# Attention in a two-layer hybrid block: scores by alternating PE row tiles, values stationary with a channel-major output, softmax divided before its transposes

## The chip, the cores and the metric

The program runs on one core of a Trainium2 chip. The metric is the device time of one execution in microseconds, the median of several runs. The engines that matter here are TensorE (PE: matmuls and transposes; PEld: its weight loads), VectorE (DVE), ScalarE (ACT) and GpSimd (POOL). Each engine works through its own list of instructions in a fixed order and waits on semaphores for the others. Matmul results go to PSUM, in banks of 512 fp32 values for each of 128 partitions.

## The reference, cut to what matters

Two layers, each a feed-forward block, a mixer with four branches, and a second feed-forward block, for 256 tokens (two blocks of 128). Two of the four branches are attention with 8 heads of 64 value channels: `mla` (96 channels in q and k, causal) and `dsa` (64 channels, one k and v shared by all heads, keys picked by an indexer). All data are fp32.

```python
def causal_dense_attention(q, k, v, scale):
    def block(args):
        s = jnp.einsum('bqhd,bshd->bhqs', qb, k).astype(jnp.float32) * scale
        s = jnp.where(kpos[None, :] <= qpos[:, None], s, -jnp.inf)
        p = jax.nn.softmax(s, axis=-1).astype(v.dtype)
        return jnp.einsum('bhqs,bshd->bqhd', p, v)
...
def dsa_branch(q, k, v, q_idx, k_idx, w_idx, cs_main, cs_idx, qk_gain):
        rel = jax.nn.relu(jnp.einsum('bqhd,bsd->bqhs', qib, k_idx).astype(jnp.float32))
        score = jnp.einsum('bqh,bqhs->bqs', wib.astype(jnp.float32), rel)
        _, sel = lax.top_k(score, topk)
        s = jnp.einsum('bqhd,bqkd->bhqk', qb, k_sel).astype(jnp.float32) * DSA_HEAD_DIM ** -0.5
        p = jax.nn.softmax(s, axis=-1).astype(v.dtype)
        return jnp.einsum('bhqk,bqkd->bqhd', p, v_sel)
...
        ys = [y_a, y_b, y_c, y_d]
        merged = gates[:, :, 0] * (y_a @ w_branch[l, 0])
        for n in range(1, N_BRANCH):
            merged = merged + gates[:, :, n] * (ys[n] @ w_branch[l, n])
```

## The kernel before, in words

Weights come from HBM in pieces of up to 512 KB (class `W`: tile `raw`, one DMA on SP's queue). ACT rounds a piece to fp32r (`hi_genexpr`, L232), DVE forms the rest (`lo_genexpr`, L103, 128x1024 elements), and every large product is three fp32r matmuls hi*hi, lo*hi, hi*lo (L244 to L246 for 256 columns, L239 to L241 for the token-major ones). Attention itself is plain fp32: one such matmul is carried out by PE in two passes, and each pass is one record in the trace.

A tile scheduler with priorities, and a table of stages, decide the order on each engine. The gate products (`ps_up_gate`) and the products with `w_branch` (`ps_up_merge`) are large matmuls that need no attention result of the moment, and they are laid between the steps of attention as filler; only the merges of `yT_dsa` and `yT_mla` wait for attention.

In each layer `attend` is called six times: for `mla` with four heads at a time (hh 0 and 1) and for `dsa` with eight heads, each for the two token blocks (tb 0 sees 128 keys, tb 1 sees 256). It works in sets of one PSUM bank, 512 score columns: four heads of 128 keys or two heads of 256. There are 12 sets in a layer. A set is:

- mask and scores on PE into a bank of `acc` (L1105, L1107; `dsa` uses 64-row tiles of the array, even heads the upper, odd heads the lower one),
- the row maximum on DVE (L1109, `mmx` or `dmx`), the exponential on ACT with its row sum (L112, `p_attend`),
- four transposes on PE (L1118, `ps_tp_attend`), copied to SBUF by ACT (L116),
- the product with the values (L1121, `ps_ms_attend`): the transposed probabilities are loaded as weights, the 64 value columns move.

After its sets, `attend` takes reciprocals of the sums and scales the token-major output (L1123 and a DVE multiply, `p_attend<-ps_ms_attend`), `y_trans` transposes it (L1133, `ps_tp_y_trans`), and it is split into hi and lo parts (`yT_mla`, `yT_dsa`). `dsa_index` forms the indexer's scores with four 32-row tiles (L1190), ACT takes relu, DVE adds the heads up.

Before the scores, k of `mla` is normalised: its sum of squares (`mkss`), a power on POOL (L321, `mkr`), two small multiplies and one of 128x512 on DVE (`s5p_mla<-...mkr_mla`), then transposes on PE (L1346). `dsc_dsa` is a similar scale for `dsa`, with a POOL step (L321) between two DVE instructions (L109, L1231).

## Time and profile before

| | before |
|---|---|
| median of 3 runs (range) | 1520.54 us (1517.99 to 1522.41) |
| profiled execution | 1519.11 us |
| its span, first to last instruction | 1517.3 us |
| granted clock of TensorE, mean | 0.982 |
| PE busy | 1439.0 us, 95% |
| DVE busy | 1167.0 us, 77% |
| ACT busy | 771.3 us, 51% |

The profiled execution is 1.8 us longer than its span and 1.4 us below the median. Attention of the first layer lies between about 433 and 529 us of the span, that of the second between about 1170 and 1266 us; both have the same structure. A timeline row gives the start, the time from the first to the last record of a run of like instructions, and in brackets the idle time of the engine ahead of it with what ended it; the step from one row's start to the next one's is what the work took.

### The profile page before, as it was taken

How to read it: one execution, taken by the hardware profiler on the slowest of the kernel's cores; microseconds unless marked ns; L12 is line 12 of the kernel's file. 1: busy time of each engine (PE TensorE's matmuls, PEld its weight loads, DVE VectorE, ACT ScalarE, POOL GpSimd, SP SyncE). 2: the span in 40 equal slices, each digit the busy share in tenths (PEclk: the TensorE clock that was granted, in tenths of full speed). 3: DMA queues.
4: the chain of work that ended last, by engine and by line, in shares of the span. 5: the costliest groups of instructions: out<-in, count | busy, mean ns of one | idle time of the engine just before them, and what ended most of it. 6: DMA issues, size and time to landing. Idle time of an engine off the chain costs nothing.

```text
span 1517.3 us, 26622 instructions
## 1 busy us (share of the span) xinstructions
PE 1439.0 (95%) x10342; PEld 1288.4 (85%) x10342; DVE 1167.0 (77%) x2003; ACT 771.3 (51%) x1223; POOL 63.6 (4%) x75
## 2 busy tenths in 40 slices
PE   8899998899989999999989998999999999999998
PEld 4588887799878897999979897889988889789997
DVE  3699978789787477988787887678987845866655
ACT  4444446644465545444454445467455655544442
POOL 0000000001010000000010000000200100000000
PEclk9999999999999999999999999999999999999999
DMA  9788888786335265899978878754642425567762
GB/s 288 232 294 285 291 258 259 203 232 172 96 102 140 70 206 175 289 320 323 321 250 257 277 244 273 229 135 135 178 132 90 124 83 158 162 212 225 235 207 98
DMA packets 241703, 313.24 MB, mean 206 GB/s; under 512 B 27704, under 2 KB 168872, under 8 KB 241576
## 3 DMA queue, kind: packets, MB, share of 16 engines
q1 hardware_dynamic: 241576, 311.53, 66.0%
q8 instruction: 81, 1.33, 0.4%
q14 instruction: 46, 0.38, 0.1%
HBM read 310.41 MB, written 1.07 MB: 205 GB/s over the span
## 4 chain that ended last, share of the span: by engine, by line
PE 62%; DVE 19%; DMA 7%; issue 5%; ACT 5%; POOL 2%; SPq 0%; POOLq 0%; DVEq 0%; ACTq 0%
DVE lo_genexpr L103 7%; PE ps_up_up_half L244 6%; PE ps_up_up_half L245 6%; PE ps_up_up_half L246 6%; PE ps_acc_down_proj L241 3%; PE ps_acc_down_proj L240 3%; PE ps_acc_down_proj L239 3%; DMA raw_init<-in_ffn_w_dram 3%; DMA raw_ada<-in_ada_w_dram 3%; PE ps_up_gate L244 3%; PE ps_up_gate L246 3%; PE ps_up_gate L245 2%; ACT hi_genexpr L232 2%; PE ps_up_merge L245 2%; PE ps_up_merge L244 2%
## 5 line engine op out<-in xcount | busy, mean ns | idle before, releaser
L232 ACT CAST hi_genexpr<-raw_init 128x1024 fp32r<-128x1024 f32 (+2 forms) x430 | 441.1, 1028 | 504.6 <-DMA raw_init<-in_ffn_w_dram 120.5
L103 DVE TENSOR_TENSOR lo_genexpr<-raw_init,hi_genexpr 128x1024 fp32r<-128x1024 f32 (+2 forms) x430 | 511.5, 1192 | 162.9 <-ACT hi_genexpr L232 155.4
L244 PE MATMUL ps_up_up_half<-uh_new_u,hi_genexpr 128*128 128x256 f32 x1216 | 339.0, 279 | 3.3 <-DVE p_silu_cols L106 2.6
L246 PE MATMUL ps_up_up_half<-uh_new_u,lo_genexpr 128*128 128x256 f32 x1216 | 337.0, 278 | 0.2 <-DVE lo_genexpr L103 0.2
L245 PE MATMUL ps_up_up_half<-ul_new_u,hi_genexpr 128*128 128x256 f32 x1216 | 337.1, 277 | 0.0
L244 PEld LDWEIGHTS ps_up_up_half<-uh_new_u,hi_genexpr 128*128 128x128 f32 x1216 | 228.5, 188 | 9.3 <-issue 7.0
L245 PEld LDWEIGHTS ps_up_up_half<-ul_new_u,hi_genexpr 128*128 128x128 f32 x1216 | 228.5, 188 | 1.4
L246 PEld LDWEIGHTS ps_up_up_half<-uh_new_u,lo_genexpr 128*128 128x128 f32 x1216 | 228.5, 188 | 0.8 <-DVE lo_genexpr L103 0.8
L106 DVE SCALAR_TENSOR_TENSOR acc_ada<-raw_ada,c_col_tile_trunk,acc_ada 128x1024 f32<-128x1024 f32 x105 | 134.4, 1280 | 28.7 <-DMA raw_ada<-in_ada_w_dram 28.3
L244 PE MATMUL ps_up_gate<-uh_new_u,hi_genexpr 128*128 128x256 f32 x512 | 145.3, 284 | 0.0
L245 PE MATMUL ps_up_gate<-ul_new_u,hi_genexpr 128*128 128x256 f32 x512 | 144.1, 281 | 0.0
L246 PE MATMUL ps_up_gate<-uh_new_u,lo_genexpr 128*128 128x256 f32 x512 | 143.6, 281 | 0.0
L239 PE MATMUL ps_acc_down_proj<-hi_genexpr,yT_mul_cols 128*128 128x512 f32 x288 | 115.7, 402 | 0.0
L241 PE MATMUL ps_acc_down_proj<-hi_genexpr,yT_mul_cols 128*128 128x512 f32 x288 | 115.6, 402 | 0.0
L240 PE MATMUL ps_acc_down_proj<-lo_genexpr,yT_mul_cols 128*128 128x512 f32 x288 | 115.3, 401 | 0.1
L244 PEld LDWEIGHTS ps_up_gate<-uh_new_u,hi_genexpr 128*128 128x128 f32 x512 | 96.5, 188 | 2.2 <-issue 1.5
L246 PEld LDWEIGHTS ps_up_gate<-uh_new_u,lo_genexpr 128*128 128x128 f32 x512 | 96.6, 189 | 0.5 <-issue 0.4
L245 PEld LDWEIGHTS ps_up_gate<-ul_new_u,hi_genexpr 128*128 128x128 f32 x512 | 96.5, 188 | 0.1
L239 PEld LDWEIGHTS ps_acc_down_proj<-hi_genexpr,yT_mul_cols 128*128 128x128 f32 x288 | 54.8, 190 | 13.3 <-issue 1.6
L240 PEld LDWEIGHTS ps_acc_down_proj<-lo_genexpr,yT_mul_cols 128*128 128x128 f32 x288 | 54.8, 190 | 12.8 <-DVE lo_genexpr L103 0.6
L241 PEld LDWEIGHTS ps_acc_down_proj<-hi_genexpr,yT_mul_cols 128*128 128x128 f32 x288 | 54.8, 190 | 12.6
L239 PE MATMUL ps_up_tok_gemm<-hi_genexpr,uh_new_u 128*128 128x424 f32 (+2 forms) x88 | 34.0, 386 | 2.2 <-ACT gt_gate L112 2.2
(476 smaller groups left out, 2750.7 us busy)
## 6 DMA issues: line engine op xcount, KB each, us to landing
raw_init<-in_ffn_w_dram SPq DMA_DIRECT2D x240, 512.0 KB
raw_ada<-in_ada_w_dram SPq DMA_DIRECT2D x128, 512.0 KB
raw_init<-in_w_in_dram SPq DMA_DIRECT2D x96, 512.0 KB
raw_init<-in_w_branch_dram SPq DMA_DIRECT2D x32, 512.0 KB
raw_init<-in_ffn_w_dram SPq DMA_DIRECT2D x36, 256.0 KB
raw_init<-in_w_out_dram SPq DMA_DIRECT2D x16, 512.0 KB
s5p_load<-in_ada_w_dram SPq DMA_DIRECT2D x16, 256.0 KB
s5p_load<-in_ada_w_dram SPq DMA_DIRECT2D x8, 512.0 KB
```

What stands on the lines that cost most here:

```text
L103: eng.tensor_tensor(o, x, y, op)
L106: V.scalar_tensor_tensor(o, x, s, y, op0, op1)
L232: S.copy(self.hi, self.raw)
L239: T.matmul(o, xh, wh, start=first, stop=False)
L240: T.matmul(o, xh, wl, start=False, stop=False)
L241: T.matmul(o, xl, wh, start=False, stop=last)
L244: T.matmul(o, wh, xh, start=first, stop=False)
L245: T.matmul(o, wh, xl, start=False, stop=False)
L246: T.matmul(o, wl, xh, start=False, stop=last)
```

## The change

1. `attend` goes through pairs of sets. For `dsa` both masks are written first, into two banks, and then the scores alternate between the two 64-row tiles and their banks. `dsa_index` alternates in the same way between its four 32-row tiles and four banks.
2. The row sums of a set are inverted and its exponentials divided (128x512 on DVE) before the transposes. The scaling after the values is gone.
3. In the product with the values, v (64 columns) is loaded as weights into one of two 64-column tiles of the array and the transposed probabilities (128 columns) move. The output is channel-major; `y_trans` is gone, and the split reads the output's bank.
4. The channels of a `dsa` output now stand in another order, so the `w_branch` pieces of branch 2 are loaded by four DMAs of a quarter each (32 DMAs in place of 8 in the program).

```diff
-            for sl, src in pieces:
-                nc.sync.dma_start(self.raw[:, :, sl], src)
+                if isinstance(src, list):
+                    for p, ks, x in src:
+                        nc.sync.dma_start(self.raw[p, ks, sl], x)
...
-        for g, hs in enumerate(r[i:i + per] for r in rows for i in range(0, len(r), per)):
-            p = bank("acc", (128, per, n))
-            T.matmul(p, identb, bc(mask[:, None, :], (128, per, n)), start=True, stop=False)
-            for i, h in enumerate(hs):
-                T.matmul(p[:, i, :], q_of(h, tb), k_of(h, n), start=False, stop=(i == per - 1))
...
-            for j, (i, h, b) in enumerate(blocks):
-                T.matmul(o[:, 64 * h:64 * h + 64], pt[:, j, :], v_of(h, b), start=(b == 0), stop=(b == tb))
-        rs = new(tag + "rs", (128, 8), bufs=2)
-        V.reciprocal(rs[:, 0:nh], sm[:, 0:nh])
-        y = new("p2", (128, nh, 64))
-        tt(y, o[:, 0:64 * nh].rearrange("p (h d) -> p h d", h=nh), bc(rs[:, 0:nh, None], (128, nh, 64)), OP.mult)
...
-        for m in range(nm):
-            T.transpose(p[:, m, :], y[:, 128 * m:128 * m + 128], ident)
...
+        for i0 in range(0, nh // step, per):
+            sets = [r[i0:i0 + per] for r in rows]
+            ps_ = [bank("acc", (128, per, n)) for _ in sets]
+            for p in ps_:
+                T.matmul(p, identb, bc(mask[:, None, :], (128, per, n)), start=True, stop=False)
+            for i in range(per):
+                for p, hs in zip(ps_, sets):
+                    T.matmul(p[:, i, :], q_of(hs[i], tb), k_of(hs[i], n), start=False, stop=(i == per - 1))
...
+                V.reciprocal(sm[:, 1, 0:per], sm[:, 0, 0:per])
+                tt(pe, pe, bc(sm[:, 1, 0:per, None], (128, per, n)), OP.mult)
...
+                    T.matmul(o[c:c + 64, m, :], v_of(h, b), pt[:, j, :], start=(b == 0), stop=(b == tb), tile_position=(0, c))
+        x = slice(tb * 128, tb * 128 + 128)
+        split(yh[:, m0:m0 + nm, x], yl[:, m0:m0 + nm, x], o)
...
-            for h0 in range(4):
-                p = bank("acc", (128, 2, n))
-                for i in range(2):
...
+            ps_ = [bank("acc", (128, 2, n)) for _ in range(4)]
+            for i in range(2):
+                for h0 in range(4):
...
+                    T.matmul(ps_[h0][:, i, :], qiT[i][o, 128 * tb:128 * tb + 128], kiT[o, 0:n], start=True, stop=True,
                              tile_position=(32 * h0, 0))
```

Three places show how the instructions stand. The first is PE at the scores of `dsa` for token block 1, first layer. Before, each of the four sets has its mask and its two heads; here are the last two sets:

```order
L1105 MATMUL ps_acc_attend_5645<-selm_dsa_index_5237,identb_tile_trunk_77 128x512
L1107 MATMUL ps_acc_attend_5645<-dkT_dsa_5137,b_dsa_5139 128x256 x2
L1105 LDWEIGHTS identb_tile_trunk_77
L1105 MATMUL ps_acc_attend_5666<-selm_dsa_index_5237,identb_tile_trunk_77 128x512
L1107 MATMUL ps_acc_attend_5666<-dkT_dsa_5137,b_dsa_5139 128x256 x2
```

After, two masks stand together, and four matmuls alternate between two banks:

```order
L1113 MATMUL ps_acc_attend_5591<-selm_dsa_index_5230,identb_tile_trunk_77 128x512
L1113 LDWEIGHTS identb_tile_trunk_77
L1113 MATMUL ps_acc_attend_5592<-selm_dsa_index_5230,identb_tile_trunk_77 128x512
L1116 MATMUL ps_acc_attend_5591<-dkT_dsa_5130,b_dsa_5132 128x256
L1116 MATMUL ps_acc_attend_5592<-dkT_dsa_5130,b_dsa_5132 128x256
L1116 MATMUL ps_acc_attend_5591<-dkT_dsa_5130,b_dsa_5132 128x256
L1116 MATMUL ps_acc_attend_5592<-dkT_dsa_5130,b_dsa_5132 128x256
```

The second pair of sets follows in the same form; the same eight matmuls are now in two runs of four. Behind them PE has 4 gate matmuls, mask and four scores of an `mla` set, 2 gate matmuls, and then the four transposes of the first `dsa` set. On DVE the maxima of the first two sets now come one after the other, then the reciprocal of the first set, the maximum of the third set, and only then the division of the first. From there to the end of attention, a set's transposes and its product with the values have 6 filler matmuls between them, and most sets have 13 or more behind them.

The second place is DVE where k of `mla` (hh 1) is scaled by the power from POOL, first layer. Before:

```order
L109 TENSOR_SCALAR mkr_mla_5324<-mkss_mla_5304 128x8
L106 SCALAR_TENSOR_TENSOR dmx_attend_5421<-dmx_attend_5421,dsc_dsa_5126 128x4
L106 SCALAR_TENSOR_TENSOR dmx_attend_5446<-dmx_attend_5446,dsc_dsa_5126 128x4
L103 TENSOR_TENSOR s5p_mla_5296<-mkp_mla_in_2758,mkr_mla_5324 128x4x32
L103 TENSOR_TENSOR lo_genexpr_5792<-raw_init_5789,hi_genexpr_5791 128x1024
L103 TENSOR_TENSOR s5p_mla_5296<-mkp_mla_in_2758,mkr_mla_5324 128x4x32
L103 TENSOR_TENSOR s5p_mla_5296<-s5p_mla_5296,mkr_mla_5324 128x8x64
```

After:

```order
L109 TENSOR_SCALAR mkr_mla_5317<-mkss_mla_5297 128x8
L106 SCALAR_TENSOR_TENSOR dmx_attend_5419<-dmx_attend_5419,dsc_dsa_5119 128x4
L106 SCALAR_TENSOR_TENSOR dmx_attend_5441<-dmx_attend_5441,dsc_dsa_5119 128x4
L103 TENSOR_TENSOR s5p_mla_5289<-mkp_mla_in_2758,mkr_mla_5317 128x4x32 x2
L103 TENSOR_TENSOR s5p_mla_5289<-s5p_mla_5289,mkr_mla_5317 128x8x64
L103 TENSOR_TENSOR lo_genexpr_5776<-raw_init_5773,hi_genexpr_5775 128x1024
L1125 RECIPROCAL dsm_attend_5423<-dsm_attend_5423 128x4
L103 TENSOR_TENSOR p_attend_5422<-p_attend_5422,dsm_attend_5423 128x512
```

One `lo_genexpr` has moved behind the three multiplies, and the division of the first `dsa` set follows it. Elsewhere on DVE, the last `mkr_mla` instruction of hh 0 now stands 12 `b_s_out` copies and one `lo_genexpr` ahead of the multiplies that wait for POOL (before, only a `MATCH_REPLACE` stood between), and the second `dsc_dsa` instruction has five others between it and the first where it had one.

The third place is PE at the end of attention, first layer. Before, gates stand between the last product with the values and the transposes of `y_trans`, and the 48 merges of `yT_dsa` follow:

```order
L1121 MATMUL ps_ms_attend_5734<-s5p_mla_5297,p_attend_5768 128x64 x4
L244 MATMUL ps_up_gate_5850<-uh_new_u_2576,hi_genexpr_5883 128x256
L245 MATMUL ps_up_gate_5850<-ul_new_u_2577,hi_genexpr_5883 128x256
L246 MATMUL ps_up_gate_5850<-uh_new_u_2576,lo_genexpr_5884 128x256
L244 MATMUL ps_up_gate_5850<-uh_new_u_2576,hi_genexpr_5883 128x256
L245 MATMUL ps_up_gate_5850<-ul_new_u_2577,hi_genexpr_5883 128x256
L1133 MATMUL ps_tp_y_trans_5782<-cst_tile_trunk_75,p_attend_5780 128x128 x2
L246 MATMUL ps_up_gate_5850<-uh_new_u_2576,lo_genexpr_5884 128x256
L244 MATMUL ps_up_merge_5918<-yT_dsa_5411,hi_genexpr_5914 128x256
```

After, the gates and nearly all merges of `yT_dsa` are used up earlier:

```order
L250 MATMUL ps_up_merge_5942<-yT_dsa_5405,hi_genexpr_5938 128x256
L1131 MATMUL ps_tp_attend_5758<-cst_tile_trunk_75,p_attend_5752 128x128 x4
L251 MATMUL ps_up_merge_5942<-yT_dsa_5404,lo_genexpr_5939 128x256
L1136 MATMUL ps_ms_attend_5720<-p_attend_5759,s5p_mla_5290 64x128 x4
L249 MATMUL ps_up_merge_5976<-yT_mla_4715,hi_genexpr_5972 128x256
L250 MATMUL ps_up_merge_5976<-yT_mla_4716,hi_genexpr_5972 128x256
```

One matmul of filler is left between the last transposes and the last product with the values, and the merges of `yT_mla`, which need that product's split, follow at once.

## Rows read from the trace of the kernel before

**Rows 1.** The page, busy time of PE: us, share, instructions.

```profile
PE 1439.0 (95%) x10342; PEld 1288.4 (85%) x10342; DVE 1167.0 (77%) x2003; ACT 771.3 (51%) x1223; POOL 63.6 (4%) x75
```

**Rows 2.** Stretches: length, busy PE, PEld, DVE, ACT, POOL; clock, DMA share, GB/s.

```profile
435.00:455.00 20.00, 19.88 (x124) 17.29 (x123) 15.49 (x41) 12.79 (x31) 2.90 (x1) 0.92 0.30 93
...
500.00:532.00 32.00, 31.89 (x247) 29.54 (x247) 13.31 (x27) 19.34 (x49) 0.00 (x0) 1.00 0.26 67
```

**Rows 3.** The chain that ended last, 425 to 490 us: start, us, what.

```profile
450.05 2.91 POOL dsc_dsa L321
...
477.52 1.09 PE ps_acc_attend L1107 x8
```

**Rows 4.** Timeline of DVE, same stretch.

```profile
432.26 0.49 DVE L103 TENSOR_TENSOR s5p_mla<-mkp_mla_in,mkr_mla 128x128 f32<-128x128 f32 x2 [1.36 <-POOL mkr_mla L321]
432.68 0.69 DVE L103 TENSOR_TENSOR s5p_mla<-s5p_mla,mkr_mla 128x512 f32<-128x512 f32 x1
...
443.25 0.17 DVE L1123 RECIPROCAL mrs_attend<-msm_attend 128x4 f32<-128x4 f32 x1
...
445.16 0.41 DVE L103 TENSOR_TENSOR p_attend<-ps_ms_attend,mrs_attend 128x256 f32<-128x256 f32 x1
...
452.99 0.17 DVE L1231 TENSOR_SCALAR dsc_dsa<-dsc_dsa 128x16 f32<-128x16 f32 x1 [2.62 <-POOL dsc_dsa L321]
...
480.10 0.69 DVE L118 COPY s5p_mla<-ps_tp_mla 96x512 f32<-96x512 f32 x1 [0.66 <-PE ps_tp_mla L1318]
...
484.42 1.22 DVE L103 TENSOR_TENSOR lo_genexpr<-raw_init,hi_genexpr 128x1024 fp32r<-128x1024 f32 x1
```

**Rows 5.** Timeline of PE at the two k transposes.

```profile
433.42 0.64 PE L1346 MATMUL ps_tp_mla<-cst_tile_trunk,s5p_mla 128*96 128x128 f32 x4 [2.59 <-DVE s5p_mla L103]
...
486.59 0.61 PE L1346 MATMUL ps_tp_mla<-cst_tile_trunk,s5p_mla 128*96 128x128 f32 x4 [1.47 <-DVE s5p_mla L103]
```

**Rows 6.** Timeline of PE within attention, 500 to 509 us.

```profile
500.13 1.13 PE L1107 MATMUL ps_acc_attend<-dkT_dsa,b_dsa 64*128 64x256 f32 x4
501.19 0.39 PE L1105 MATMUL ps_acc_attend<-selm_dsa_index,identb_tile_trunk 128*128 128x512 bf16 x1
501.51 1.13 PE L1107 MATMUL ps_acc_attend<-dkT_dsa,b_dsa 64*128 64x256 f32 x4
...
507.06 1.00 PE L1121 MATMUL ps_ms_attend<-dc_dsa_in,p_attend 128*128 128x64 f32 x8
507.89 0.61 PE L1118 MATMUL ps_tp_attend<-cst_tile_trunk,p_attend 128*128 128x128 f32 x4
508.34 0.38 PE L1105 MATMUL ps_acc_attend<-maskb_tile_trunk,identb_tile_trunk 128*128 128x512 bf16 x1
```

**Rows 7.** Timeline of PE where small tiles of the array are used.

```profile
379.69 0.28 PE L245 MATMUL ps_up_gate<-ul_new_u,hi_genexpr 128*128 128x256 f32 x1
379.81 0.28 PE L246 MATMUL ps_up_gate<-uh_new_u,lo_genexpr 128*128 128x256 f32 x1
380.01 0.64 PE L812 MATMUL ps_acc_s_out_prep<-s5p_s_out_prep,s5bd_s_prep 128*32 128x128 f32 x16
380.47 0.24 PE L815 MATMUL ps_acc_s_out_prep<-p_s_out_prep,cst_tile_trunk 128*32 128x32 f32 x8
...
382.15 0.73 PE L1190 MATMUL ps_acc_dsa_index<-dki_dsa_index,s_dsa_index 32*128 32x128 f32 x12
383.33 0.71 PE L1190 MATMUL ps_acc_dsa_index<-dki_dsa_index,s_dsa_index 32*128 32x128 f32 x4 [0.45 <-ACT p_dsa_index L112]
```

**Rows 8.** Weight loads of the 32-column tiles: min, median, max ns.

```profile
L812 PEld LDWEIGHTS ps_acc_s_out_prep<-s5p_s_out_prep,s5bd_s_prep x128: 106/110/113, 380.0 to 1119.1; 128*32 128x32 f32 x128
```

**Rows 9.** Timeline of ACT: two exponentials of a set, and one copy.

```profile
504.21 0.57 ACT L112 ACTIVATE p_attend<-ps_acc_attend,dmx_attend,dsc_dsa 128x256 f32<-128x256 f32 x1
...
504.76 0.56 ACT L112 ACTIVATE p_attend<-ps_acc_attend,dmx_attend,dsc_dsa 128x256 f32<-128x256 f32 x1
...
506.18 0.59 ACT L116 COPY p_attend<-ps_tp_attend 128x512 f32<-128x512 f32 x1 [0.76 <-PE ps_tp_attend L1118]
```

More of the change, by code (lines that the diff above doesn't have):

```diff
@@ L1128, in y_trans @@
-    def y_trans(tb, y, nh, m0, yh, yl):
-        nm = nh // 2
-        p = bank("tp", (128, nm, 128))
-        y = y.rearrange("p h d -> p (h d)")
-        for m in range(nm):
-            T.transpose(p[:, m, :], y[:, 128 * m:128 * m + 128], ident)
-        x = slice(tb * 128, tb * 128 + 128)
-        split(yh[:, m0:m0 + nm, x], yl[:, m0:m0 + nm, x], p)
+        for i0 in range(0, nh // step, per):
[6 more added lines that the diff above has]
+                    T.matmul(p[:, i, :], q_of(hs[i], tb), k_of(hs[i], n), start=False, stop=(i == per - 1))
+            for g, (p, hs) in enumerate(zip(ps_, sets)):
+                mx = new(tag + "mx", (128, 2, 4), bufs=2)
+                V.tensor_reduce(mx[:, 0, 0:per], p, AX.X, OP.max)
+                stt(mx[:, 1, 0:per], mx[:, 0, 0:per], -1.0, sc[:, hs[0]:hs[-1] + 1:step], OP.mult, OP.mult)
+                pe = new("p2", (128, per, n))
+                sm = new(tag + "sm", (128, 2, 4), bufs=2)
+                for i, h in enumerate(hs):
+                    act(pe[:, i, :], p[:, i, :], AF.Exp, bias=mx[:, 1, i:i + 1], scale=sc[:, h:h + 1], accum=sm[:, 0, i:i + 1])
+                V.reciprocal(sm[:, 1, 0:per], sm[:, 0, 0:per])
+                tt(pe, pe, bc(sm[:, 1, 0:per, None], (128, per, n)), OP.mult)
+                tp = bank("tp")
+                pt = new("p2", (128, 4, 128))
+                blocks = [(i, h, b) for b in range(tb + 1) for i, h in enumerate(hs)]
+                for j, (i, h, b) in enumerate(blocks):
+                    T.transpose(tp[:, 128 * j:128 * j + 128], pe[:, i, 128 * b:128 * b + 128], ident)
+                cp(pt.rearrange("p j s -> p (j s)"), tp, KN["p"][(i0 + g) % 2])
+                for j, (i, h, b) in enumerate(blocks):
+                    m = h % step * (nh // 2 // step) + h // step // 2
+                    c = 64 * (h // step % 2)
+                    T.matmul(o[c:c + 64, m, :], v_of(h, b), pt[:, j, :], start=(b == 0), stop=(b == tb), tile_position=(0, c))
@@ L1184, in dsa_index @@
             first = True
[L1185 to L1190 removed]
+            ps_ = [bank("acc", (128, 2, n)) for _ in range(4)]
+            for i in range(2):
+                for h0 in range(4):
+                    o = slice(32 * h0, 32 * h0 + 32)
+                    T.matmul(ps_[h0][:, i, :], qiT[i][o, 128 * tb:128 * tb + 128], kiT[o, 0:n], start=True, stop=True,
                              tile_position=(32 * h0, 0))
+            for h0, p in enumerate(ps_):
                 rel = new("p2", (128, 2, n))
@@ L1251, in dsa @@
             o = lambda h: slice(64 * (h % 2), 64 * (h % 2) + 64)
-            y = attend(tb, 8, 2, lambda h, t: qT[o(h), h // 2, 128 * t:128 * t + 128], lambda h, n: kT[o(h), 0:n],
-                       lambda h, b: zc[:, b, 64:128], masks[tb], sc[:, tb], "d")
-            show(f"dsay{l}{tb}", y)
-            y_trans(tb, y, 8, 0, yh, yl)
+            attend(tb, 8, 2, lambda h, t: qT[o(h), h // 2, 128 * t:128 * t + 128], lambda h, n: kT[o(h), 0:n],
+                   lambda h, b: zc[:, b, 64:128], masks[tb], sc[:, tb], "d", yh, yl, 0)
             yield
```

38 lines of the change are left out of this document (14 added, 24 removed).

## The prediction

> **What bounds the kernel now.** The page comes first: PE is busy for 95% of the span, DVE for 77% [rows 1], so work taken off PE pays wherever PE is not waiting for someone. The stretches tell where that is. From 500 to 532 us of the first layer PE is busy for 31.89 of 32 us, DVE for 13.31 and ACT for 19.34, at full clock [rows 2]: this is the second half of attention, and PE alone sets its pace. Before about 487 us it is different. PE is full from 435 to 455 us too (19.88 of 20), but DVE has 15.49 [rows 2], and the chain that ended last goes through DVE and POOL there: a POOL step of 2.91 us at 450 us is a piece of it [rows 3]. The timeline of PE shows two waits at the k transposes of `mla`: 2.59 us at 433 us and 1.47 us at 486 us, both ended by DVE [rows 5]. So I cost the change in two parts: ahead of 487 us by what it does to DVE's list, behind it by what it takes off PE. The second layer repeats the first; I work one layer and double it.
>
> **The product with the values.** Today it is 8 records of 128*128 that take 0.83 us from start to start [rows 6], 0.10 for each pass, though only 64 columns move. The new form has four matmuls, again 8 passes, with 128 columns moving, in two column tiles by turns. The trace has no tile of 64 columns. The nearest is `s_out_prep`: 16 records of 128*32 with 128 moving columns take 0.46 us [rows 7], four tiles at once, so a round of tiles takes 0.11. With two tiles, 8 passes are four rounds, 0.46. Changing the tile shape costs something: the full-array matmul ahead of that row starts 0.20 before it, and the like of it ahead of that took 0.12 [rows 7], so about 0.09 is spent going in, and I assume the same going out. That makes 0.46 + 0.18 = 0.64, or 0.2 less in each set. Bounds: at best the shape change hides and 0.37 is gained; at worst two tiles don't overlap, 8 x 0.115 + 0.18 = 1.10, and 0.27 is lost. I take 0.2 because the nearest row is a column tile. 12 sets are 2.4 us, 9 of them (1.8) behind 487 us.
>
> The Trainium skill ("TensorEngine Tiling (Array Packing)", Key Properties and Restrictions) speaks against this part: a change of the tiling mode drains TensorE, and column tiling disables Fast Weight Load. In this trace a weight load of a 32-column tile takes 0.110 us [rows 8], and 16 of them fit beside the 16 matmuls of the 0.46 us row [rows 7]; that overlap agrees with another sentence there, that different tiles load and multiply in parallel. Were slow loads to serialise, the sum would be that of the first rival below.
>
> **`y_trans`.** Four transposes take 0.45 us [rows 6]. 16 a layer go; 12 of them, 1.35 us, lie behind 487 us.
>
> **Scores of `dsa`, token block 1.** A set's four passes take 1.06 us (500.13 to 501.19) and its mask 0.32 [rows 6]: 5.5 us for four sets. Row tiles do overlap when their matmuls stand next to each other and have banks of their own: 12 records of the indexer on three tiles take 0.73 us [rows 7] where one by one they would take about 12 x 0.11 = 1.3. A pass of 256 columns is (1.06 - 0.18) / 4 = 0.22 of that. A pair of sets becomes 0.22 + 0.32 for the masks and two passes' time twice, 4 x 0.22 + 0.1 going out: 1.5, so 3.0 for both pairs. Gain 2.5; at least 0.4 (only the shape changes saved), at most 2.7, if going in and out is hidden too. I take 2.3, since the turns of the two tiles may not line up.
>
> **Scores of `dsa`, token block 0.** 8 passes of 128 columns take 1.09 us for each set [rows 3]; two sets in one are about 1.1 less. This lies ahead of 487 us, and DVE's copy of the transposed q waits 0.66 us for PE just there [rows 4]. I count 0.6.
>
> **The division.** Each set gets a reciprocal (0.17) and a 128x512 multiply (0.69) on DVE [rows 4]: 0.86 for 12 sets, against the reciprocals and the six multiplies that go (0.41 for 128x256 [rows 4], about 0.69 for 128x512). That is some 6 us more on DVE in a layer. Behind 487 us DVE has room: 13.31 of 32 us are busy [rows 2]. Ahead of it, three sets add 2.6 and take 1.2 away, +1.4 net. It also lengthens the way of a set: the transposes now wait for reciprocal and multiply.
>
> **DVE's order.** The idle 1.36 us that DVE waits for POOL ahead of the k multiplies at 432 us [rows 4] goes, as copies and a `lo_genexpr` now fill it: 1.4 gained. The 2.62 us wait in `dsc_dsa` [rows 4] gets about 2.3 us of other work into it; less the +1.4 of the division, 0.9 gained. At 484.42 a `lo_genexpr` of 1.22 us [rows 4] stood between the multiplies of k; it moves behind them, 1.2 gained. If the waits only move on to the next instruction that needs PE or ACT, these three are worth nothing. With 0.6 of the scores and 0.4 for products and transposes that the chain passes through on PE at 457 to 460 us, the part ahead of 487 us gains 4.5.
>
> **New waits.** (1) The first `dsa` set of token block 1: from its scores' end to its transposes come two maxima and a small one (about 1.5, a maximum costing about as much as a 128x512 multiply), two exponentials (0.55 from start to start, so 1.2 [rows 9]), a reciprocal, the third set's maximum and the multiply (1.5): about 4.4 with the hand-overs. PE has the other pair (1.5), an `mla` set (1.1) and six gates (0.7), 3.3. It waits 1.1. (2) Later sets: copy 0.59, exponentials 1.2 [rows 9], reciprocal and multiply 0.86, hand-overs 0.15, together 2.8, against 6 fillers, product, and 13 fillers (0.7 + 0.64 + 1.5 = 2.8): even. (3) The end: one filler stands between the last transposes and the last product, so PE waits for the 0.59 copy, about 0.6; then the merges of `yT_mla` wait for the split, of which the first six matmuls' worth (0.7) is covered: 0.2. Together +1.9.
>
> **At nothing.** The indexer's fourth tile waited 0.45 us for its bank [rows 7]; that is far ahead of the k waits, which absorb it. The four-way weight DMAs: DMA is busy 0.26 of the time where they land [rows 2]. If that cover were gone, one late piece would cost about its extra issue time, below 1 us.
>
> **Sum.** Behind 487 us: 1.8 + 1.35 + 2.3 = 5.45 gained. Ahead: 4.5. New waits: 1.9. That is 8.05 a layer, 16.1 in all: 1519.1 - 16.1 = 1503.0 for the profiled execution, and 1.4 more for the median: **1504**.
>
> **The rivals.** (A) Two column tiles of 64 don't overlap, because weight loads take turns: 0.46 more in each set, 5.5 a layer, 11 in all: 1515. For it: nothing in the trace has this shape. Against it: [rows 7]. (B) The waits of point (2) don't even out, because the division stands in DVE's list behind a `lo_genexpr` of 1.22 us [rows 4] when it falls due. Then each of the 10 sets behind 455 us makes PE wait for its division and reciprocal (0.86) and about half of a `lo_genexpr` (0.6), 1.5 us: 15 a layer in place of the 1.1 of point (1), so the layer loses 13.9 - 8.05 = 5.85, and the time is 1532. The sign turns where a set waits for more than 0.9. For it: the loop through ACT, DVE and PE is closed in each set, as ACT copies one set before it takes the next one's exponentials. Against it: the fillers come to the same length, and DVE is idle for over half of that time [rows 2]. (C) More is gained: the waits of (1) and (2) vanish since fillers suffice, and the clock holds. It stands at 0.92 from 435 to 455 us [rows 2], that is, in part at 1.2 in place of 2.4 GHz, behind the 2.59 us wait [rows 5]; with 1.4 of that wait gone, 20 x 0.08 = 1.6 us may come back in each layer. That would be 1.6 + 1.1 a layer: 1499. (D) PE loses its work but the time doesn't move, as the chain is DVE's throughout: 1518 to 1521. Against it: PE's full 32 us behind 500 us [rows 2].
>
> **How the numbers follow.** My sum 0.50 (1499 to 1510), (C) 0.18, (A) 0.14, (B) 0.10, (D) 0.08. A measurement of this kernel tells about 0.3%, 4.6 us, from no change. Faster by more: the sum, (C), and most of (A), 0.78. Within: (D) and the rest of (A), 0.12. Slower: 0.10, from (B). The range 1493 to 1516 holds the sum, (C) and most of (A).
>
> **What would show it.** Right: 8 records of the new product from 0.5 to 0.7 us apart from what follows; four alternating scores in about 1 us; no `y_trans`; waits at the k transposes near 1.2 us (hh 0) and smaller (hh 1); a new idle of about 1 us ahead of the first transposes of `dsa` token block 1 and 0.6 at attention's end. Wrong: the products at 0.9 or more (A); PE idle by 0.5 or more ahead of most sets' transposes, ended by DVE (B); the same length from 435 to 487 us with PE idle in place of busy (DVE's gains only moved).

## The result and the profile after

| | before | after |
|---|---|---|
| median (range), 4 runs each on one chip | 1519.3 us (1517.99 to 1522.41) | 1497.94 us (1495.38 to 1499.71) |
| ratio, 95% interval | | 0.9855 [0.9833, 0.9878] |
| profiled execution, its span | 1519.11, 1517.3 us | 1495.38, 1493.6 us |
| granted clock of TensorE in it, mean | 0.982 | 0.990 |

The kernel is 21.4 us faster by the medians; 16.1 were forecast. The changed kernel was run again twice on other chips, at 0.9872 and 0.9856.

The page of the changed kernel, busy time of each engine (us, share, instructions), beside [rows 1]:

```profile
PE 1413.4 (95%) x10310; PEld 1262.7 (85%) x10310; DVE 1175.4 (79%) x2027; ACT 770.0 (52%) x1223; POOL 64.0 (4%) x75
```

PE is busy for 25.6 us less, DVE for 8.4 more. Not all of the 25.6 is work: at a lower clock the same matmuls keep PE busy for longer. By the mean clocks (0.018 of the one span and 0.010 of the other are lost) some 12 us of it are clock, an estimate. The span is 23.7 us shorter, about what PE's busy time lost, so PE's idle time did not shrink (78.3 us before, 80.2 after). It moved.

Next, one mixer cut into seven stages at marks that both kernels have: from the first scores of the indexer to the first large product of `mla`, from there to the first transposes of q (hh 0), of k (hh 0), of `dsa`, of q (hh 1), of k (hh 1), and to the first record behind the mixer. The columns are those of [rows 2]. First the kernel before (the fifth and sixth stage, left out, are 13.6 and 10.9 us long):

```profile
381.90:394.80 12.90, 9.97 (x100) 8.51 (x88) 11.18 (x33) 8.15 (x20) 0.96 (x1) 0.96 0.42 124
394.80:415.70 20.90, 20.90 (x147) 20.40 (x146) 14.09 (x52) 7.68 (x16) 1.65 (x1) 0.86 0.17 52
415.70:433.20 17.50, 13.90 (x96) 12.14 (x94) 15.91 (x34) 11.84 (x20) 1.64 (x1) 1.00 0.45 142
433.20:461.90 28.70, 27.75 (x179) 24.34 (x180) 23.48 (x67) 17.09 (x41) 2.90 (x1) 0.94 0.35 101
...
486.40:561.80 75.40, 75.07 (x596) 70.36 (x597) 41.37 (x60) 41.14 (x81) 0.00 (x0) 1.00 0.44 132
```

The same seven stretches of the changed kernel:

```profile
382.50:394.40 11.90, 9.67 (x97) 8.40 (x88) 10.06 (x28) 7.83 (x19) 0.96 (x1) 1.00 0.45 133
394.40:414.40 20.00, 20.00 (x150) 19.46 (x148) 15.09 (x56) 8.17 (x17) 1.65 (x1) 0.91 0.20 58
414.40:430.60 16.20, 13.94 (x95) 12.03 (x93) 15.91 (x34) 10.51 (x18) 1.86 (x1) 1.00 0.49 149
430.60:458.10 27.50, 26.34 (x189) 23.05 (x190) 26.18 (x71) 19.39 (x44) 2.90 (x1) 1.00 0.37 105
458.10:469.50 11.40, 10.07 (x74) 8.95 (x72) 9.68 (x21) 7.57 (x14) 1.81 (x1) 1.00 0.71 186
469.50:478.50 9.00, 7.24 (x63) 6.42 (x63) 7.39 (x18) 3.87 (x13) 1.64 (x1) 1.00 0.42 117
478.50:552.60 74.10, 71.53 (x596) 65.52 (x596) 46.68 (x71) 42.01 (x82) 0.00 (x0) 1.00 0.45 134
```

Every stage is shorter, this mixer by 9.8 us and that of the second layer by 11.7 at the same marks. Some filler changed places, so raw lengths must be read with that: 12 gate matmuls (1.4 us) went from the sixth stage to the last, and 12 merges from the fifth to the fourth. With that put back, the last stage is about 3 us shorter (75.4 - 74.1 + 1.4 = 2.7; in the second layer 3.1), where the prediction had 5.45 less its waits of 1.9, that is 3.55. The fourth to sixth stages are 53.2 - 47.9 - 1.4 = 3.9 shorter, and some 1.5 of that is clock (3.4 us at half speed are gone, below). The first three, in which the prediction had only the 1.4 of the k wait at their end, are 51.3 - 48.1 = 3.2 shorter. In the last stage PE is idle for 2.6 us where it was for 0.3, and DVE is busier by 5.3: work left PE, and part of it came back as waiting.

The timeline of PE after, the work that the change touches. It answers to [rows 6]:

```profile
483.23 0.28 PE L249 MATMUL ps_up_gate<-uh_new_u,hi_genexpr 128*128 128x256 f32 x1
483.53 0.66 PE L1136 MATMUL ps_ms_attend<-p_attend,dc_dsa_in 128*64 128x128 f32 x8
484.12 0.39 PE L250 MATMUL ps_up_gate<-ul_new_u,hi_genexpr 128*128 128x256 f32 x1
...
489.24 0.61 PE L1113 MATMUL ps_acc_attend<-selm_dsa_index,identb_tile_trunk 128*128 128x512 bf16 x2
489.78 1.14 PE L1116 MATMUL ps_acc_attend<-dkT_dsa,b_dsa 64*128 64x256 f32 x8
490.85 0.61 PE L1113 MATMUL ps_acc_attend<-selm_dsa_index,identb_tile_trunk 128*128 128x512 bf16 x2
```

The product with the values takes 0.59 us to the next start (483.53 to 484.12) in place of 0.83, with 0.30 from the gate ahead of it (0.12 to 0.30 before). A pair of sets of scores takes 1.61 (489.24 to 490.85); two sets apart took 2.76, 1.06 + 0.32 each.

The waits of PE in the same stretch, of 0.9 us and more, without the q wait (1.58). They answer to [rows 5]:

```profile
430.79 0.64 PE L1349 MATMUL ps_tp_mla<-cst_tile_trunk,s5p_mla 128*96 128x128 f32 x4 [1.07 <-DVE s5p_mla L103]
450.84 0.63 PE L1131 MATMUL ps_tp_attend<-cst_tile_trunk,p_attend 128*128 128x128 f32 x4 [0.94 <-DVE p_attend L103]
...
478.73 0.61 PE L1349 MATMUL ps_tp_mla<-cst_tile_trunk,s5p_mla 128*96 128x128 f32 x4 [1.50 <-DVE s5p_mla L103]
494.31 0.38 PE L1113 MATMUL ps_acc_attend<-maskb_tile_trunk,identb_tile_trunk 128*128 128x512 bf16 x1 [1.12 <-ACT p_attend L112]
523.70 0.66 PE L1136 MATMUL ps_ms_attend<-p_attend,s5p_mla 128*64 128x128 f32 x8 [1.06 <-ACT p_attend L116]
```

The k wait of hh 0 fell from 2.59 to 1.07, that of hh 1 stayed (1.47 and 1.50), and three waits are new: 0.94 ahead of the third `mla` set, 1.12 ahead of a mask, 1.06 ahead of the last product.

The indexer's first twelve records, on three tiles, take about as long as before (0.73 us, [rows 7]), though the tiles now take turns:

```profile
382.71 0.72 PE L1194 MATMUL ps_acc_dsa_index<-dki_dsa_index,s_dsa_index 32*128 32x128 f32 x12
```

So the row tiles overlapped as well when they came one after the other. What the edit changed lies elsewhere, in the waits.

On DVE, the instruction behind the POOL step of `dsc_dsa` waits 1.03 us where it waited 2.62. The k multiplies of hh 1 wait 1.61 us for POOL in both kernels; here are the row of before and the two rows of after:

```profile
484.21 0.29 DVE L103 TENSOR_TENSOR s5p_mla<-mkp_mla_in,mkr_mla 128x128 f32<-128x128 f32 x1 [1.61 <-POOL mkr_mla L321]
```

```profile
448.62 0.17 DVE L1236 TENSOR_SCALAR dsc_dsa<-dsc_dsa 128x16 f32<-128x16 f32 x1 [1.03 <-POOL dsc_dsa L326]
477.49 0.49 DVE L103 TENSOR_TENSOR s5p_mla<-mkp_mla_in,mkr_mla 128x128 f32<-128x128 f32 x2 [1.61 <-POOL mkr_mla L326]
```

From there to the k transposes it is 2.38 us before (484.21 to 486.59, with the `lo_genexpr` of [rows 4] between) and 1.24 after (477.49 to 478.73). DVE's way got 1.1 us shorter, but PE's wait at its end did not, since twelve gates that stood ahead of it now stand behind it and are done in the last stage, where PE is the limit.

Last, the clock. In the first layer's mixer of these two profiles, three stretches show TensorE at about half of full speed, that is at 1.2 in place of 2.4 GHz (columns as in [rows 2]). Before, the first begins behind a wait of the indexer, the second behind the k wait; after, only the first is left, half as long:

```profile
393.66:400.49 6.83, 6.83 (x24) 6.06 (x23) 5.43 (x22) 3.64 (x9) 0.00 (x0) 0.52 0.27 78
434.62:438.03 3.41, 3.41 (x14) 2.88 (x13) 2.47 (x3) 1.89 (x3) 0.00 (x0) 0.53 0.23 77
```

```profile
394.21:397.62 3.41, 3.41 (x12) 3.00 (x11) 3.23 (x14) 1.97 (x6) 0.00 (x0) 0.53 0.54 154
```

### The profile page after: what moved, and what is told of

Same layout as the page of the kernel before. It is cut to its first block, busy times and chain, and to the rows that moved or that the text cites. A ratio compares the mean times of both kernels' runs of the same rounds, so it can differ in the third digit from the quotient of the medians.

```text
span 1493.6 us, 26644 instructions
## 1 busy us (share of the span) xinstructions
PE 1413.4 (95%) x10310; PEld 1262.7 (85%) x10310; DVE 1175.4 (79%) x2027; ACT 770.0 (52%) x1223; POOL 64.0 (4%) x75
## 3 DMA queue, kind: packets, MB, share of 16 engines
HBM read 310.41 MB, written 1.07 MB: 209 GB/s over the span
## 4 chain that ended last, share of the span: by engine, by line
PE 55%; DVE 21%; DMA 11%; issue 6%; ACT 5%; POOL 1%; SPq 1%; POOLq 0%; DVEq 0%; ACTq 0%
DVE lo_genexpr L103 7%; DMA raw_ada<-in_ada_w_dram 5%; PE ps_up_up_half L249 5%; PE ps_up_up_half L250 5%; PE ps_up_up_half L251 5%; DMA raw_init<-in_ffn_w_dram 4%; PE ps_acc_down_proj L246 3%; PE ps_acc_down_proj L245 3%; PE ps_acc_down_proj L244 3%; PE ps_up_gate L250 3%; ACT hi_genexpr L237 3%; PE ps_up_gate L249 3%; PE ps_up_gate L251 3%; DVE acc_ada L106 2%; PE ps_up_merge L250 2%
## 5 line engine op out<-in xcount | busy, mean ns | idle before, releaser
L246 PEld LDWEIGHTS ps_acc_down_proj<-hi_genexpr,yT_mul_cols 128*128 128x128 f32 x288 | 54.1, 188 | 12.3
```

What stands on the lines that cost most here:

```text
L246: T.matmul(o, xl, wh, start=False, stop=last)
```

## The experiments

The theory: PE's lighter attention gives most of the gain. The rivals: the gain is the indexer's, which the prediction had at nothing; or the clock's, since waits became shorter. Each run below is compared with the kernel before on the same chip; ratios are given with a 95% interval.

Since the mean granted clock differs from run to run of one kernel, the runs can also be compared at one clock. Over all runs, time falls by 1.22 us for each 0.001 of mean granted clock, with 2.0 us of scatter left (one slope for all kernels). "At equal clock" below means moved along that slope to 0.985. It is arithmetic over runs, not an experiment of its own, and a difference of two kernels by it is good to 1 to 2 us. Before stands there at 1516.8 us (its mean clock is 0.9817), after at 1501.8 (0.9873).

### One part alone

**e1_scores**: the kernel before, with only the scores of `dsa` alternating.

```diff
-            p = bank("acc", (128, per, n))
-            T.matmul(p, identb, bc(mask[:, None, :], (128, per, n)), start=True, stop=False)
-            for i, h in enumerate(hs):
-                T.matmul(p[:, i, :], q_of(h, tb), k_of(h, n), start=False, stop=(i == per - 1))
...
+            for p in ps_:
+                T.matmul(p, identb, bc(mask[:, None, :], (128, per, n)), start=True, stop=False)
+            for i in range(per):
+                for p, hs in zip(ps_, sets):
+                    T.matmul(p[:, i, :], q_of(hs[i], tb), k_of(hs[i], n), start=False, stop=(i == per - 1))
```

> The kernel before with one part of the change: the dsa scores of two sets alternate between the two row tiles (masks first); indexer, division and values as before. Work theory (the time follows the matmul time taken off PE): pairs of sets for token block 1 take 1.6 us in place of 2 x 1.38, so 2.3 us a layer, and 1.1 for token block 0: 6.8 us in all, some 1512. Clock theory (much of the whole gain is TensorE's granted clock): the same half-clock stretches as before stay (two of 6.8 us right behind the indexer's wait, at 394 and 1131 us), and no more than 6.8 us is gained. Order theory (the gain ahead of 487 us is DVE's new order, not PE's work): less than 3 us.

Measured: 1517.5 us, 0.9976 [0.995, 1.0003]; 2.7 us at equal clock. PE's timeline in it:

```profile
483.38 0.61 PE L1322 MATMUL ps_tp_mla<-cst_tile_trunk,s5p_mla 128*96 128x128 f32 x4 [1.69 <-DVE s5p_mla L103]
493.50 0.61 PE L1350 MATMUL ps_tp_mla<-cst_tile_trunk,s5p_mla 128*96 128x128 f32 x4 [1.75 <-DVE s5p_mla L103]
508.42 0.44 PE L1122 MATMUL ps_tp_attend<-cst_tile_trunk,p_attend 128*128 128x128 f32 x2 [0.46 <-ACT p_attend L112]
```

The q wait (1.69 for 1.46) and the k wait (1.75 for 1.47 in [rows 5]) grow, and a set's transposes wait 0.46: of 3.4 us a layer taken off PE (2.3 + 1.1), 1 comes back as waiting right there. Alone, this part is worth two fifths of what PE saves; where the rest of the difference went, this run does not show. It moves the masks ahead and lets the scores take turns in one edit. As the indexer's tiles overlapped without taking turns, the gain may be the masks' new place alone; no run parts the two.

**e2_index**: the kernel before, with only the indexer's four row tiles alternating.

```diff
-            for h0 in range(4):
-                p = bank("acc", (128, 2, n))
-                for i in range(2):
...
+            ps_ = [bank("acc", (128, 2, n)) for _ in range(4)]
+            for i in range(2):
+                for h0 in range(4):
...
```

> The kernel before with the indexer's four row tiles alternating, nothing else. Work theory: 0.3 us a layer, so at most 0.6 in all, no measurable change. Clock theory: the wait for the fourth bank gets about 0.9 us shorter (2.5 to 1.5 us), the half-clock stretches right behind it (6.8 us each, at 394 and 1131 us) get shorter or vanish, and 2 to 6 us are gained.

Measured: 1512.6 us, 0.9946 [0.9921, 0.9971]; 4.2 at equal clock. The prediction had 0. The second and third stage, columns as above:

```profile
397.20:417.20 20.00, 20.00 (x150) 19.56 (x148) 15.09 (x56) 8.17 (x17) 1.64 (x1) 0.91 0.20 57
417.20:433.40 16.20, 13.96 (x95) 12.07 (x93) 15.88 (x34) 10.50 (x18) 1.86 (x1) 1.00 0.50 151
```

They are those of the changed kernel, nearly to the digit, and not those of before (20.90 at clock 0.86, 17.50). In PE's timeline the indexer's wait and the k wait of hh 0 have the changed kernel's lengths too:

```profile
396.33 1.12 PE L1189 MATMUL ps_acc_dsa_index<-dki_dsa_index,s_dsa_index 32*128 32x256 f32 x4 [1.54 <-ACT p_dsa_index L112]
433.62 0.64 PE L1346 MATMUL ps_tp_mla<-cst_tile_trunk,s5p_mla 128*96 128x128 f32 x4 [1.07 <-DVE s5p_mla L103]
```

So the shorter k wait of hh 0 belongs to the indexer's edit, which changes the order on DVE far behind it, and not to `attend`: in this run, too, twelve `b_s_out` copies and a `lo_genexpr` stand ahead of the k multiplies, and these no longer wait for POOL.

**e3_divide**: the kernel before, with only the division ahead of the transposes. The late multiply becomes a copy; `y_trans` stays.

```diff
...
+            V.reciprocal(dv[:, 0:per], sm[:, hs[0]:hs[-1] + 1:step])
+            tt(pe, pe, bc(dv[:, 0:per, None], (128, per, n)), OP.mult)
             tp = bank("tp")
...
-        tt(y, o[:, 0:64 * nh].rearrange("p (h d) -> p h d", h=nh), bc(rs[:, 0:nh, None], (128, nh, 64)), OP.mult)
+        V.tensor_copy(y, o[:, 0:64 * nh].rearrange("p (h d) -> p h d", h=nh))
```

> The kernel before with the division moved ahead of the transposes (reciprocal and 128x512 multiply in each of 12 sets a layer); the output's multiply becomes a plain copy of the same size, y_trans stays. Work theory: 12 x 0.86 = 10 us more on DVE a layer, mostly beside a full PE; 0 to 4 us slower in all. Rival B of the prediction (each division is waited for): 1 us for each of 24 sets, 20 us slower or more.

Measured: 1537.7 us, 1.0103 [1.0073, 1.0134]; 9.6 slower at equal clock. PE's timeline has new waits behind DVE:

```profile
456.53 0.39 PE L245 MATMUL ps_up_merge<-yT_s_glu,hi_genexpr 128*128 128x256 f32 x1 [1.77 <-DVE yT_s_glu L106]
...
536.22 0.44 PE L1134 MATMUL ps_tp_y_trans<-cst_tile_trunk,p_attend 128*128 128x128 f32 x2 [0.52 <-DVE p_attend L1126]
538.28 0.55 PE L244 MATMUL ps_up_merge<-yT_mla,hi_genexpr 128*128 128x256 f32 x1 [1.62 <-DVE p_merge L106]
```

Early division by itself is a loss. These waits add up to 3.9 us a layer, where before had 0.36 in the first place and less than 0.3 in the others. At the end of attention (the last two rows) the copy, `y_trans` and the split stand one behind the other with nothing left to fill them, and the change takes two of these three away; the first row lies elsewhere. That the shorter end is what makes the division bearable in the changed kernel is argued from these rows and not tested alone.

**e4_values**: the changed kernel, with scores and indexer in the order of before (the two diffs above, the other way round, but the sets still come with even and odd heads by turns). What is left is values stationary, channel-major output, early division.

> The changed kernel with the scores and the indexer put back into the order of before, so values stationary, channel-major output and early division alone. Work theory: 0.23 us a set and 1.75 us of y_trans a layer, 9 us in all, less the waits for the division (0 to 4): 1510 to 1514. Clock theory: the half-clock stretches behind the indexer's wait are there as before. If the row-tile order is all that counts: no gain or a loss.

Measured: 1516.5 us, 0.9979 [0.9959, 0.9999]; 7.7 at equal clock. Its mean clock is 0.9786, lower than before's, so most of the gain doesn't show. PE's timeline shows where:

```profile
457.42 1.09 PE L1129 MATMUL ps_tp_attend<-cst_tile_trunk,p_attend 128*128 128x128 f32 x4 [2.85 <-DVE p_attend L103]
```

A division falls due late in DVE's list, PE waits 2.85 us for it (2.97 in the second layer), and the fourth stage has 6.8 us at half clock, 3.4 behind the k wait as before and 3.4 behind this one; so has the second layer's. The parts at equal clock are 2.7 + 4.2 + 7.7 = 14.6, the whole is 15.1: they add up within their errors, and the clock comes on top.

### One part less, or done otherwise

**e9_noindex**: the changed kernel with the indexer's old order (e2's diff the other way round).

> The changed kernel with the indexer alone put back into its old order (three tiles' matmuls, then a wait, one tile after the other). Theory that the indexer's alternation gave a third of the gain: at full clock the stretch from the index scores to mla's products is 0.5 to 0.9 us longer in each layer, the stretch between the q and k transposes of hh 0 goes from 16.2 back to 17.5 us, the k wait from 1.1 to 2.6 us, and half-clock stretches come back behind it; 5 to 10 us slower than the changed kernel. Prediction's theory (the indexer is worth nothing): no change.

Measured: 1510.43 us, 0.993 [0.9903, 0.9957], against 0.9872 and 0.9856 for the changed kernel. At equal clock it is 11.2 below before, so the indexer gives 3.9 of 15.1; the other 8.4 of the 12.3 between the mean times is clock (0.9804 to 0.9873). PE's timeline has the two long waits of before again, and e4's wait for a division:

```profile
393.94 1.68 PE L1195 MATMUL ps_acc_dsa_index<-dki_dsa_index,s_dsa_index 32*128 32x256 f32 x4 [2.41 <-ACT p_dsa_index L112]
433.91 0.64 PE L1349 MATMUL ps_tp_mla<-cst_tile_trunk,s5p_mla 128*96 128x128 f32 x4 [2.60 <-DVE s5p_mla L103]
454.86 0.63 PE L1131 MATMUL ps_tp_attend<-cst_tile_trunk,p_attend 128*128 128x128 f32 x4 [2.85 <-DVE p_attend L103]
```

and its second and fourth stages are at 0.86 and 0.89 of the clock, where the changed kernel has 0.91 and 1.00:

```profile
395.30:416.20 20.90, 20.90 (x147) 20.37 (x146) 14.11 (x52) 7.67 (x16) 1.64 (x1) 0.86 0.18 52
...
433.70:464.50 30.80, 27.55 (x173) 23.72 (x174) 24.56 (x70) 17.09 (x40) 2.90 (x1) 0.89 0.33 94
```

Without the indexer's edit the mean clock stays where before had it (0.9804 and 0.9817), and of the 21.9 us between the mean times of before and of the changed kernel, 9.6 are left.

**e6_bank**: the changed kernel, the indexer's fourth tile in a bank of `ms`, so that it waits for none of the first three.

```diff
-            ps_ = [bank("acc", (128, 2, n)) for _ in range(4)]
+            ps_ = [bank("ms" if h0 == 3 else "acc", (128, 2, n)) for h0 in range(4)]
```

> The changed kernel, with the indexer's fourth row tile writing to the bank of ms, which is free then, in place of a fourth bank of acc, so that all eight index matmuls of a token block run at once without the wait for ACT's relu (1.5 us for block 1 and 0.7 for block 0). Theory that the indexer's wait matters by the clock behind it and by DVE's start: 1 to 2 us a layer at full clock and no half-clock stretch behind the index, 2 to 6 us faster than the changed kernel. Theory that the k waits absorb it (the prediction's): no change.

Measured: 1496.88 us, 0.9862 [0.9834, 0.9889], beside 0.9872 [0.9838, 0.9905] for the changed kernel on the same chip (**e5_after**): no difference that can be told. The wait has only moved on to the next product, which needs a bank of `acc`:

```profile
392.24 0.45 PE L244 MATMUL ps_acc_mla<-hi_genexpr,mlh_mla_in 128*128 128x384 f32 x1 [3.23 <-ACT p_dsa_index L112]
```

> The changed kernel once more, on the chip of the next three runs. All theories: 0.985 of before. Work theory: at full clock throughout, a layer's mixer (from the indexer's first score to the next norm) is 7 us shorter than before's, and the rest of the difference is half-clock time; so if this chip grants both kernels the same clock, only some 14 us are gained.

**e10_bank2**: two of the four tiles elsewhere, so that this wait goes too.

```diff
-            ps_ = [bank("acc", (128, 2, n)) for _ in range(4)]
+            ps_ = [bank(t, (128, 2, n)) for t in ("acc", "acc", "tp", "ms")]
```

> The changed kernel with two of the indexer's four tiles writing to the banks of tp and ms, so that two acc banks stay free for mla's products that follow. If the 3.2 us wait ahead of those products (with one tile moved to ms) is for an acc bank: it shrinks to below 1.5 us, 1.5 to 2.5 us a layer gained at full clock, and no half-clock stretch behind it: 4 to 8 us faster than the changed kernel. If mla's products wait for relu's results through something else than a bank: no change against one tile moved.

Measured: 1510.85 us, 0.9938 [0.9915, 0.996], beside 0.9856 for the changed kernel on the same chip. At equal clock it would be the faster one (17.9 below before, against 15.1), but none of its runs reached that clock (0.982 at most). The stretches tell what happened (the first is the whole first stage, 7.6 us for 11.9):

```profile
378.60:386.20 7.60, 7.60 (x99) 7.14 (x88) 5.91 (x17) 4.32 (x12) 0.96 (x1) 1.00 0.45 138
386.20:390.00 3.80, 1.82 (x16) 1.32 (x9) 3.61 (x11) 2.84 (x6) 0.00 (x0) 1.00 0.48 140
390.00:413.90 23.90, 23.90 (x107) 23.47 (x106) 12.85 (x48) 6.62 (x16) 1.64 (x1) 0.50 0.16 45
```

Behind a wait of 1.98 us PE works without a gap for 23.9 us at half clock, in both layers. The first stage is 4.3 us shorter, and this wait gives 2.0 of them back; the half clock takes some 12, half of the 23.9.

**e12_after**, the changed kernel beside it: 1498.68 us, 0.9856 [0.9831, 0.988]. Its profiled execution, at 1507.76 the longest of its six, has such a stretch too, in the first layer alone, behind an indexer's wait of 1.60 us like that of the changed kernel's first profile. So has e1's, the longest of its thirteen (1528.72), behind a wait of 2.48. The row of e12, then that of e1:

```profile
388.00:415.30 27.30, 27.30 (x116) 26.29 (x115) 12.96 (x48) 6.64 (x16) 1.64 (x1) 0.51 0.13 39
```

```profile
393.40:420.70 27.30, 27.30 (x116) 26.27 (x115) 12.33 (x46) 6.31 (x15) 1.65 (x1) 0.50 0.14 39
```

> The changed kernel again, on the chip of these three runs, as their base: 0.985 to 0.987 of before.

**e7_nodiv**: the changed kernel without the reciprocals and the division.

```diff
-                V.reciprocal(sm[:, 1, 0:per], sm[:, 0, 0:per])
-                tt(pe, pe, bc(sm[:, 1, 0:per, None], (128, per, n)), OP.mult)
```

> The changed kernel without the reciprocal and the multiply of the division (the softmax is left undivided). Cover theory: the division is hidden beside PE, so the time stays within 4 us of the changed kernel. Wait theory: the new waits (0.9 us at 451, 1.1 at 494 and 1.1 at 523 us) and a part of the stretch from the k transposes of hh 0 to those of dsa are the division's; 2 to 5 us a layer are gained, 4 to 10 us in all.

Measured: 1494.77 us, 0.9839 [0.9808, 0.9871]; 4.2 below the changed kernel at equal clock, 24 sets, so 0.17 us a set. The new wait of token block 1 is still there, and of nearly the same length:

```profile
493.35 0.33 PE L1129 MATMUL ps_tp_attend<-cst_tile_trunk,p_attend 128*128 128x128 f32 x1 [0.94 <-ACT p_attend L112]
```

So it is the exponentials' and not the division's. The other two new waits, 0.94 ahead of the third `mla` set and 1.06 ahead of the last product, are gone: these two are the division's, 2.0 us a layer, about the 4.2.

**e8_cols**: the changed kernel, the product's matmuls sorted by column tile instead of by turns.

```diff
-                for j, (i, h, b) in enumerate(blocks):
+                for j, (i, h, b) in sorted(enumerate(blocks), key=lambda e: e[1][1] // step % 2):
                     m = h % step * (nh // 2 // step) + h // step // 2
```

> The changed kernel with the products with the values sorted by column tile (both matmuls of one 64-column tile, then both of the other) in place of by turns. Overlap theory: the two tiles work at once only when their matmuls alternate; sorted, a product takes 0.9 to 1.0 us in place of 0.6, 0.35 x 24 sets, up to 8 us slower. Other theory: the gain of the product comes from moving 128 columns past 64 weights in fewer passes, whatever the order, or the engine looks ahead far enough: no change.

Measured: 1500.3 us, 0.9876 [0.9849, 0.9903], the same as the changed kernel beside it (0.9872). The product takes 0.59 or 0.60 us in either order:

```profile
482.13 0.67 PE L1136 MATMUL ps_ms_attend<-p_attend,dc_dsa_in 128*64 128x128 f32 x8
482.73 0.38 PE L250 MATMUL ps_up_gate<-ul_new_u,hi_genexpr 128*128 128x256 f32 x1
```

By itself that fits the other theory of the expectation as well, in which the gain needs no overlap. The single records of the trace decide: in both kernels the eight start in four pairs 0.1 to 0.16 us apart, and the two of a pair start 7 ns apart by turns (483.534 and 483.541) and 13 ns apart when sorted (482.135 and 482.148). The two tiles work at the same time in either order.

**e11_dma**: the kernel before, with the weights of branch 2 loaded in four quarters (same rows, same order).

```diff
+                if n == 2:
+                    src = [(slice(64 * s_, 64 * s_ + 64), slice(2 * a_, 2 * a_ + 2), src[64 * s_:64 * s_ + 64, 2 * a_:2 * a_ + 2, :])
+                           for s_ in range(2) for a_ in range(2)]
```

> The kernel before with the branch 2 pieces of w_branch loaded by four DMAs of a quarter each, in their old order of rows; nothing else. All theories: no change (within 0.2%), since DMA has room there. If late weights matter: PE idle ahead of the merges of yT_dsa, 1 us or more a layer.

Measured: 1520.03 us, 0.9987 [0.9961, 1.0013]. The DMAs cost nothing, as the prediction had it.

## Why the prediction was right, and which step was not

The range (1493 to 1516) holds the time, and by size the sum was near: 16.1 us forecast, 15.1 measured at equal clock. The remaining 6.8 us of mean gain go with the clock (0.9817 to 0.9873 at 1.22 us for 0.001), so the time, 1497.9, lies below the sum's own 1499 to 1510 and next to rival C's 1499.

That the sum is so near is in part luck: its terms were off both ways. At equal clock the scores gave 2.7 (e1) where 5.8 were forecast (2.3 and 0.6 a layer). Product, `y_trans` and early division together gave 7.7 (e4) for 3.3 (3.6, 2.7 and 0.8, less 3.8 of new waits). The indexer gave 4.2 (e2) for nothing, and DVE's order, forecast at 7.0, has no part of its own in the runs. Without the indexer's edit the mean gain is 9.6 us (e9).

The rows tell more simply what carries the result, for a layer at full clock. PE has 8.0 us less to do (0.23 in each of 12 products, 1.8 of `y_trans`, 3.4 of scores), the waits of the indexer and of k are 2.2 shorter, and three new waits take 3.1. That is 7.1 a layer, some 14 us in all. Point by point:

- **The product with the values.** 0.64 forecast, 0.59 found; from the gate ahead to the gate behind, with the step into it, 0.87 for 1.10 before (means over a layer): 0.23 a set where 0.2 was taken. Rival A is out: the two tiles' records start 7 ns apart (13 in e8), and so do their weight loads (6 and 14 ns).
- **Scores of `dsa`.** A pair of sets was to take 1.5 us and takes 1.61. PE's saving is there, but a faster stretch of PE runs into the next wait, which the step left out: alone (e1) it gave 2.7 of 6.8 us at equal clock, and about 2 of the 4.1 that are missing are seen in longer waits.
- **The indexer, "At nothing".** This step failed. It said that the fourth tile's wait of 0.45 us lies far ahead of the k waits, "which absorb it". It looked at token block 0 alone. For token block 1 the trace of before has this row, ten microseconds later:

```profile
393.43 1.64 PE L1190 MATMUL ps_acc_dsa_index<-dki_dsa_index,s_dsa_index 32*128 32x256 f32 x4 [2.48 <-ACT p_dsa_index L112]
```

  That wait fell to 1.54 us, and that of token block 0 rose from 0.45 to 0.69. The k wait did not absorb the 0.7 that this leaves: it fell too, by 1.5. Together that is 2.2 us a layer, and e2 and e9 put the edit at 4 us of 15 at equal clock. Inside the whole it is worth 12 us of mean time, the rest being clock. The half clock behind the indexer's own wait is not the safe part of this: 6.83 us fell to 3.41 in the first layer of these two profiles, but over all profiles the stretch is 6.83 or longer in 10 of 12 layers behind the long wait (2.4 to 2.5 us: before, e1, e3, e4, e9, e11) and still in 7 of 12 behind the short one (1.5 to 1.6: the changed kernel three times, e2, e7, e8).
- **DVE's order.** The 1.4 at the k wait of hh 0 came (2.59 to 1.07), but from the indexer's edit (e2 has it, e9 loses it). The `dsc_dsa` wait fell by 1.6 (2.62 to 1.03) where 2.3 of work was to go into it; neither e2 (2.68) nor e9 (2.62) nor e7 (2.62) has that, so it takes the indexer's edit and the division. The 1.2 of the moved `lo_genexpr` came on DVE (2.38 to 1.24 us from POOL's end to the k transposes), and so did the 0.66 that DVE's copy of q waited for PE. But PE's wait there stayed at 1.5 us: the shorter stage holds twelve gates less, and the 1.4 us that they take went to the last stage, where PE is the limit. Here a shorter chain on DVE gained only what it took off PE's idle time; the prediction counted all of it, and its own doubt (waits that only move on) was the better guess here.
- **New waits.** (1) 1.1 was forecast and 1.12 found, at a mask instead of the transposes and ended by the exponentials on ACT. Its reason was off, since without the division (e7) 0.94 of it stays. (2) Even, as forecast: between 496 and 522 us no set of the changed kernel waits. (3) 0.8 forecast, 1.06 found, ended by the copy that it named; but without the division it is gone (e7), so it is the division that makes this copy late. Unforeseen: 0.94 ahead of the third `mla` set, for a division. DVE's own added work was 4.2 us a layer (8.4 in all), not 6. Rival B is out for this change (0.17 us a set in e7, its turning point was 0.9), but e3 shows the like of it: with token-major output and `y_trans` kept, early division costs 0.6% at equal clock.
- **The clock** stood in rival C alone, as 1.6 us a layer; the sum had nothing for it. The fourth stage did go from 0.94 to 1.00, as C had it. In the profiles of the six kernels with the long k wait (before, e1, e3, e4, e9, e11), the granted clock over the 8 us behind that wait (2.57 to 2.60 us) was 0.79 in 10 of 12 layers; in the other eight profiles, behind waits of 0.92 to 1.07 us, it was 1.00 in all 16. C's other half is refuted: the wait of (1) did not vanish. C had the k wait's 1.4 and the clock behind it right, but both came by the edit that the prediction had at nothing.

What stays open: why the half clock ends after 3.4 us in one execution and after 23.9 or 27.3 in another. The wait's length does not order them: behind 3.2 us (e6) it was 3.4 in both layers, behind 2.0 (e10) 23.9 in both, behind 1.5 to 1.6 anything from nothing to 27.3. No run here tells these apart. No variant here that keeps the division is measurably faster than the changed kernel.

## What to carry to other kernels

List every wait of the engine that bounds the kernel, in each repeat of a step, and not the first one only: the wait that mattered here stood in token block 1 of a step whose token block 0 looked harmless. Cost an edit also by what it does to the order far behind it, and try it alone, since the parts' gains added up at equal clock here, while the clock depended on which waits were left and was not foretold by their length. A stage that is shortened runs into the next wait, and filler that no longer fits into it must be done elsewhere, so name both before counting the gain.
